# Seven-product pairs of an MLP: two accumulations continue in the banks of two others, five vector sums instead of seven

## The chip, the cores and the metric

The kernel runs on one core of one Trainium2 chip. The metric is device time in microseconds (us), the median of the runs shown. TensorE is called PE in the profile, VectorE DVE, ScalarE ACT, GpSimd POOL, SyncE SP; PEld is the loading of weights into PE. PSUM, the memory that PE writes, has eight banks here, each of which holds one result of 128 x 512 fp32 numbers.

## The reference

A decoder trunk of two layers on 256 tokens with a residual stream of 2048 numbers, all in fp32: attention with latent projections (MLA) and an MLP, then a Mamba-2 mixer and an MLP. Each of the four parts begins with an RMS norm and adds its result to the stream. The change lies in the MLPs:

```
def squared_relu_mlp(h, w_in, w_out):
    u = jax.nn.relu(h @ w_in)
    return (u * u) @ w_out
...
h = rms_norm(x, mlp_norm_g[i])
x = x + squared_relu_mlp(h, mlp_w_in[i], mlp_w_out[i])
```

with `w_in` of 2048 x 8192 and `w_out` of 8192 x 2048.

## The kernel before, in words

*fp32 by halves.* Every operand of a large product is split into a high half and a low half (`Flow.halves`, lines 102 and 103): ACT copies the raw weights, rounded, into `wh`, and DVE writes the difference into `wl`. A product of 128 x 128 by 128 x 512 then takes three matmuls, high by high, high by low and low by high (lines 616 to 618). Weights come in units of 128 x 1024 numbers (512 KB). A unit is loaded into one of six `raw` buffers by SP's queue, and split into one of four `wh` and one of four `wl` buffers. `Flow.next` loads units up to six ahead of the one that PE takes next, and splits them three ahead.

*The hidden layer in pairs.* The 8192 hidden columns are 16 blocks of 512, taken as eight pairs p. Pair 0 is computed classically. Pairs 1 to 7 are computed with seven products instead of eight: the tokens are two halves (t = 0, 1), the contraction is two halves, the columns are two blocks (j = 0, 1). The seven products M1, M2, N3, N4, N5, N6 and N7 have combinations of the activations on one side (made once per MLP, `combinations`) and of the weights on the other (made per unit on DVE at line 183, and on POOL's queue by a load that adds, line 199). Each product is four units of six matmuls. The four results come out of them by sums: with w = N6 - M1,

```
(j0, t0) = M1 + M2            (j1, t1) = N7 + N5 + w
(j0, t1) = N4 - (N7 + w)      (j1, t0) = N5 + N3 + w
```

*Banks.* N7 accumulates in a bank of the pool `sm` (2 banks, shared with the transposes); the other six take a bank of `acc` (4 banks) each when their first unit begins. `yp` (2 banks) holds the output product.

*After a product* (`after`, line 627): M1 is copied to SBUF by ACT (line 630). When both N5 and N6 are complete, DVE makes w, `c` = N5 + w, N7 + w and `e` = N7 + c; when N4, M2 or N3 is complete, one more DVE sum makes the result. `sub` is line 620 and `plus` line 621. ACT then scales and applies the ReLU (`relu_in_place`, line 624), squares (line 566), and `turn` enters the transposes of the result into a list of due times. From pair 1 to 6, POOL's queue first copies three quarters of the squared result (line 308). PE transposes them (lines 322 and 324), ACT and DVE split the transposed result (lines 299 and 300).

*Order.* PE runs in the order in which the program is written, which `plan` and `merged` make: units of the seven products, in the order of M1, N7, N5, N6 by quarter, then N4, then M2, then N3, with units of the output product (`o`, from the hidden pairs before) put in between by estimates of PE's and DVE's work. A pair's last unit of N3 is followed by two units of `o`, then by the next pair's M1 and N7, one more unit of `o`, and its N5 and N6. In pair 7, N3 follows N6 more closely, and four units of `o` come at its end. The other engines' instructions are put in order by the framework from dependencies and estimates, so that instructions that stand together in the program may be interleaved with splits. Every engine then runs its own queue in order.

Of the kernel before, what the change touches and what calls it, by code (L numbers as in the profile page):

```python
# [23 lines left out]
AF = mybir.ActivationFunctionType  # L24
# [5 lines left out]
S = 256  # L30
# [184 lines left out]
class Trunk:  # L215
# [343 lines left out]
    def mlp_body(self, mp, layer, gain):  # L559
        nc = self.nc  # L560
        xa, rs = self.xT, self.rs
        us = {}

        def hidden(r, pp, j, t):

            nc.scalar.activation(r, r, AF.Square)
            if (pp, j) not in us:
                us[pp, j] = (self.ktile(self.k4), self.ktile(self.k4))
            h, lo = us[pp, j]
            if by_words(pp, j, t):  # L570
                r = self.words(r, 3, mp)
            return lambda wide: self.transposes(r, h, lo, t, wide)

        def relu(src, t):
            r = self.scratch()
            nc.scalar.activation(r, src, AF.Relu, scale=rs[t])
            return r

        def lhs_x(kt, t):
            return [v[:, kt % 8] for v in xa[kt // 8, t]]  # L580

        def lhs_u(pp):
            return self.from_tiles([us[pp, 0], us[pp, 1]])

        S, steps = self.combinations(mp, xa)
        S["M1"], S["N4"], S["M2"] = xa[0, 0], xa[1, 1], xa[1, 0]
        out, bank, v, count = {}, {}, {}, {}
        due = []
        at = [0.0, 0.0]

        def when(us, fn):
            due.append((at[0] + us, fn))

        def move(us):
            at[0] += us
            for e in [e for e in due if e[0] <= at[0]]:
                due.remove(e)
                e[1]()

        def turn(r, p, j, t, us):  # L600

            fn = hidden(r, p, j, t)
            at[1] = max(at[0] + us + (COPY if by_words(p, j, t) else 0), at[1] + TR_GAP)
            due.append((at[1], lambda: fn(False)))

        def pair_of_banks(pool):
            return [pool.tile([P, 512], F32, tag=pool.name, name=self.name(pool.name)) for _ in range(2)]

        def products(accs, key, lhs, kt, first, last):
            u, (h, lo) = self.flow.next(key)  # L610
            for q in range(2):
                k = 2 * kt + q
                wh, wl = h[:, q * 512:(q + 1) * 512], lo[:, q * 512:(q + 1) * 512]
                for t, b in enumerate(accs):
                    ah, al = lhs(k, t)
                    nc.tensor.matmul(b, ah, wh, start=first and q == 0, stop=False)  # L616
                    nc.tensor.matmul(b, ah, wl, start=False, stop=False)  # L617
                    nc.tensor.matmul(b, al, wh, start=False, stop=last and q == 1)  # L618

        sub = lambda o, a, b: nc.vector.tensor_tensor(o, a, b, ALU.subtract)  # L620
        plus = lambda o, a, b: nc.vector.tensor_tensor(o, a, b, ALU.add)

        def relu_in_place(r, t):
            nc.scalar.activation(r, r, AF.Relu, scale=rs[t])
            return r

        def after(name, p):
            if name == "M1":
                v["m1"] = self.scratch()
                nc.scalar.activation(v["m1"], bank["M1"], AF.Copy)  # L630
            elif name in ("N5", "N6"):
                v[name] = p
                if v.get("N5") != p or v.get("N6") != p:
                    return
                w, c, e = (self.scratch() for _ in range(3))
                sub(w, bank["N6"], v["m1"])
                plus(c, bank["N5"], w)
                plus(w, bank["N7"], w)
                plus(e, bank["N7"], c)
                v["w"], v["c"] = w, c  # L640
                turn(relu_in_place(e, 1), p, 1, 1, TR[0])
            elif name == "N4":
                sub(v["w"], bank["N4"], v["w"])
                turn(relu_in_place(v["w"], 1), p, 0, 1, TR[1])
            elif name == "M2":
                plus(v["m1"], bank["M2"], v["m1"])
                turn(relu_in_place(v["m1"], 0), p, 0, 0, TR[2])
            elif name == "N3":
                plus(v["c"], bank["N3"], v["c"])
                turn(relu_in_place(v["c"], 0), p, 1, 0, TR[3])  # L650

        tokens = plan()
        inside = False
        when(5, steps[0])
        when(10, steps[1])
        for tok in tokens:
            key = (tok[0], layer) + tok[1:]
            if tok[0] == "s":
                _, p, name, d = tok
                if not inside:  # L660
                    inside = True
                    self.flow.ahead = (6, 3)
                if count.setdefault(name, 0) % 4 == 0:
                    pool = self.sm if name == "N7" else self.acc
                    bank[name] = pool.tile([P, 512], F32, tag=pool.name, name=self.name("st"))
                count[name] += 1
                products([bank[name]], key, lambda k, t: [x[:, k] for x in S[name]], d,
                         count[name] % 4 == 1, count[name] % 4 == 0)
                if count[name] % 4 == 0:
                    after(name, p)  # L670
                move(1.36)
            elif tok[0] == "c":
                _, p, j, o = tok
                if o == 0:
                    out["c"] = pair_of_banks(self.yp if j else self.acc)
                products(out["c"], key, lhs_x, o, o == 0, o == 7)
                if o == 7:
                    for t in range(2):
                        turn(relu(out["c"][t], t), p, j, t, TR[4])
                    if j:  # L680
                        when(3, steps[2])
                if o % 2:
                    self.tick()
                move(2.72)
            else:
                _, p, nb, o = tok
                if o == 0:
                    out[nb] = pair_of_banks(self.yp)
                products(out[nb], key, lhs_u(p), o, o == 0, o == 3)
                if o == 3:  # L690
                    self.add_residual(nb, out.pop(nb))
                move(2.72)
        move(1e9)
        assert not self.queue
        if gain is not None:
            self.boundary_begin(gain)
        for nb in range(4):
            keys = [("mo", layer, 7, nb, q) for q in range(2)]
            if gain is None and nb == 3:
                self.last_block(keys, lhs_u(7))  # L700
                break
            accs = self.block(keys, lhs_u(7))
            if gain is not None:
                self.finalize(nb, accs)
            else:
                for t in range(2):
                    self.result(t, nb, slice(0, 512), accs[t])
        if gain is not None:
            self.boundary_end()
# [694 lines left out]
TR = (10, 8, 7, 7, 5)  # L1404
# [4 lines left out]
def by_words(p, j, t):  # L1409

    return 0 < p < 7
# [48 lines left out]
def plan():  # L1460

    out = [("c", 0, 0, o) for o in range(8)]
    for p in range(1, 8):
        first = [(("o", p - 2, 3), 4)] if p > 1 else [(("c", 0, 1), 8)]
        out += merged(p, first + [(("o", p - 1, nb), 4) for nb in range(4 if p == 7 else 3)])
    return out
# [139 lines left out]
```

## Time and profile before

| what | us |
|---|---|
| median of 3 runs (lowest to highest) | 2285.71 (2285.32 to 2286.46) |
| the profiled execution: span from its first to its last instruction (its time beside that is not listed) | 2284.5 |
| PE busy | 2278.1 |
| PEld busy | 1889.6 |
| DVE busy | 1915.9 |
| ACT busy | 1390.1 |
| POOL busy | 275.5 |

The first MLP takes about 257 to 905 us of the span, the second about 1592 to 2240 us. In a row of a group stand: line, engine, operation, result <- operands by the program's names (`st` is a bank of one of the seven products, `s` a scratch tile, `sN` the combined activations, `xt` activations as they are, `wraw` a weight buffer), shapes, count, busy time, mean length in ns, and the engine's idle time just before, with what ended it. In a row of a timeline stand start, length, engine, line and operation; in a row of the chain of waits, start, length and what. Matmuls are pipelined: a record is longer than the step from one start to the next.

### The profile page before, as it was taken

To read this page: it belongs to the slowest core of one execution; us is meant where nothing else is said; L and a number is where in the kernel's file an instruction comes from. 1 tells how busy PE (TensorE), PEld (TensorE's weight loads), DVE (VectorE), ACT (ScalarE), POOL (GpSimd) and SP (SyncE) were. 2 spreads that over 40 slices of the span, in tenths; PEclk is the share of its full clock that TensorE was granted. 3 is DMA by queue.
4 is the path that set the end of the run, shared out by engine and by line. 5 is a ranking of instruction groups with operands and counts; after the bars stand their busy time and mean duration, and the time that the engine had idled before them with its cause. 6 is when DMAs were issued, how large, how long until landed. Compare 5 with 4: busy or idle time off the path is not lost.

```text
span 2284.5 us, 30768 instructions
## 1 busy us (share of the span) xinstructions
PE 2278.1 (100%) x10929; PEld 1889.6 (83%) x10929; DVE 1915.9 (84%) x2318; ACT 1390.1 (61%) x1947; POOL 275.5 (12%) x315
## 2 busy tenths in 40 slices
PE   9999999999999999999999999999999999999999
PEld 7898888888888888888888888888888888888887
DVE  7786698999898897687899688676989889989985
ACT  7775576566666666564666555545666666666663
POOL 1440000000000000100133213121000000000000
PEclk9999999999999999999999999999999999999999
DMA  8545678888888878667888787767688888888874
GB/s 315 173 153 159 211 230 267 259 255 270 264 255 259 267 232 271 227 208 241 277 280 278 245 275 264 229 222 229 204 265 248 259 270 253 260 275 247 267 232 160
DMA packets 167706, 557.16 MB, mean 244 GB/s; under 512 B 19040, under 2 KB 28192, under 8 KB 166528
## 3 DMA queue, kind: packets, MB, share of 16 engines
q1 hardware_dynamic: 151264, 502.44, 66.2%
q0 software_dynamic: 13888, 48.49, 10.0%
q10 hardware_dynamic: 2400, 4.27, 0.5%
q8 instruction: 86, 1.41, 0.3%
q14 instruction: 68, 0.56, 0.1%
HBM read 529.65 MB, written 6.41 MB: 235 GB/s over the span
## 4 chain that ended last, share of the span: by engine, by line
PE 96%; DVE 1%; DMA 1%; ACT 1%; issue 1%; POOL 0%; SPq 0%; ACTq 0%; DVEq 0%
PE acc L339 13%; PE acc L340 13%; PE acc L343 13%; PE yp L618 9%; PE yp L617 9%; PE yp L616 9%; PE st L617 7%; PE st L618 7%; PE st L616 7%; DMA wraw<-mi 1%; PE sm L324 1%; DVE wl L103 1%; PE y L1309 1%; PE sm L322 1%; PE acc L616 1%; PE acc L618 1%
## 5 line engine op out<-in xcount | busy, mean ns | idle before, releaser
L102 ACT ACTIVATE wh<-wraw 128x1024 fp32r<-128x1024 f32 (+1 forms) x818 | 856.2, 1053 | 570.4 <-PE acc L340 268.9
L103 DVE TENSOR_TENSOR wl<-wraw,wh 128x1024 fp32r<-128x1024 f32 (+1 forms) x818 | 985.5, 1221 | 240.6 <-ACT wh L102 216.6
L616 PE MATMUL yp<-wh,k 128*128 128x512 f32 x896 | 349.2, 390 | 0.0
L618 PE MATMUL yp<-wh,k 128*128 128x512 f32 x896 | 348.8, 389 | 0.0
L617 PE MATMUL yp<-wl,k 128*128 128x512 f32 x896 | 348.6, 389 | 0.0
L339 PE MATMUL acc<-wh,xt 128*128 128x512 f32 x704 | 279.7, 397 | 0.4 <-ACT wh L102 0.4
L340 PE MATMUL acc<-wh,xt 128*128 128x512 f32 x704 | 274.9, 390 | 0.1
L102 ACT ACTIVATE wh<-wrx 128x1024 fp32r<-128x1024 f32 x168 | 177.8, 1058 | 153.4 <-PE yp L618 101.7
L103 DVE TENSOR_TENSOR wl<-wrx,wh 128x1024 fp32r<-128x1024 f32 x168 | 204.3, 1221 | 36.6 <-ACT wh L102 35.6
L618 PEld LDWEIGHTS yp<-wh,k 128*128 128x128 f32 x896 | 168.2, 188 | 35.1
L617 PEld LDWEIGHTS yp<-wl,k 128*128 128x128 f32 x896 | 168.2, 188 | 34.9
L616 PEld LDWEIGHTS yp<-wh,k 128*128 128x128 f32 x896 | 168.2, 188 | 34.8
L339 PE MATMUL acc<-wh,k 128*128 128x512 f32 x496 | 196.5, 396 | 0.0
L340 PE MATMUL acc<-wh,k 128*128 128x512 f32 x496 | 193.3, 390 | 0.0
L343 PE MATMUL acc<-wl,xt 128*128 128x512 f32 x704 | 188.3, 389 | 0.0
L616 PE MATMUL st<-wh,xt 128*128 128x512 f32 x448 | 177.7, 397 | 0.0
L618 PE MATMUL st<-wh,xt 128*128 128x512 f32 x448 | 174.9, 390 | 0.0
L617 PE MATMUL st<-wl,xt 128*128 128x512 f32 x448 | 174.7, 390 | 0.0
L339 PEld LDWEIGHTS acc<-wh,xt 128*128 128x128 f32 x704 | 132.7, 188 | 29.4 <-ACT wh L102 1.6
L340 PEld LDWEIGHTS acc<-wh,xt 128*128 128x128 f32 x704 | 132.5, 188 | 28.5 <-issue 1.2
L343 PEld LDWEIGHTS acc<-wl,xt 128*128 128x128 f32 x704 | 132.1, 188 | 27.7
L199 POOL DMA_DIRECT2D wrx<-mi x56 | 49.2, 878 | 720.6 <-DVE wl L103 524.5
(318 smaller groups left out, 3527.0 us busy)
## 6 DMA issues: line engine op xcount, KB each, us to landing
wraw<-mi SPq DMA_DIRECT2D x256, 512.0 KB, 5.5
wraw<-mo SPq DMA_DIRECT2D x256, 512.0 KB, 5.6
wraw<-si SPq DMA_DIRECT2D x160, 512.0 KB, 5.2
wraw<-so SPq DMA_DIRECT2D x64, 512.0 KB, 5.2
wrx<-mi SPq DMA_DIRECT2D x56, 512.0 KB, 5.4
wrx<-mi POOLq DMA_DIRECT2D x56, 512.0 KB, 7.8
wraw<-wo SPq DMA_DIRECT2D x32, 512.0 KB, 4.0
taps<-xD SPq DMA_DIRECT2D x16, 768.0 KB, 8.4
```

Source lines behind the costliest of these rows:

```text
L102: self.last = nc.scalar.activation(h[:, v], raw[:, v], AF.Copy)
L103: self.last_lo = nc.vector.tensor_tensor(lo[:, v], raw[:, v], h[:, v].bitcast(F32), ALU.subtract)
L199: nc.gpsimd.dma_start(st["b11"].tile, quarter(d, 1, 0), accum_op=ALU.add)
L322: self.nc.tensor.transpose(b.bitcast(F32R)[:, v], words[:, v], self.ident_r)
L324: self.nc.tensor.transpose(b[:, v], src[:, v], self.ident)
L339: nc.tensor.matmul(accs[t][:, :n], ah, wh[:, q, :], start=first and kt + q == 0, stop=False)
L340: nc.tensor.matmul(accs[t][:, :n], al, wh[:, q, :], start=False, stop=False)
L343: nc.tensor.matmul(accs[t][:, :n], lhs(kt + q, t)[0], wl[:, q, :], start=False, stop=en and q == nk - 1)
L616: nc.tensor.matmul(b, ah, wh, start=first and q == 0, stop=False)
L617: nc.tensor.matmul(b, ah, wl, start=False, stop=False)
L618: nc.tensor.matmul(b, al, wh, start=False, stop=last and q == 1)
L1309: nc.tensor.matmul(y[t][c, o], part(t)[:, c], xg[g][t][:, o], start=True, stop=True)
```

## The change

M2 no longer takes a bank: its products go on accumulating in M1's bank, after ACT has copied M1 out, and ACT applies the ReLU to that bank directly. N3 goes on in N5's bank after the sums that need N5 have been read. The sums behind N5 and N6 become w = N6 - M1, `g` = N7 + w and `e` = N5 + g; with the one behind N4 and the one behind N3 they are five for a pair. Such continued accumulations begin without the flag that starts a sum, and their group check at build time is skipped (`more`). A pair takes four banks of `acc` in place of six. Plan, order of products, weights and due times are the same.

```diff
-        def products(accs, key, lhs, kt, first, last):
+        def products(accs, key, lhs, kt, first, last, more=False):
...
-                    nc.tensor.matmul(b, ah, wh, start=first and q == 0, stop=False)
-                    nc.tensor.matmul(b, ah, wl, start=False, stop=False)
-                    nc.tensor.matmul(b, al, wh, start=False, stop=last and q == 1)
+                    nc.tensor.matmul(b, ah, wh, start=first and q == 0, stop=False, skip_group_check=more)
+                    nc.tensor.matmul(b, ah, wl, start=False, stop=False, skip_group_check=more)
+                    nc.tensor.matmul(b, al, wh, start=False, stop=last and q == 1, skip_group_check=more)
...
-                w, c, e = (self.scratch() for _ in range(3))
+                w, g, e = (self.scratch() for _ in range(3))
                 sub(w, bank["N6"], v["m1"])
-                plus(c, bank["N5"], w)
-                plus(w, bank["N7"], w)
-                plus(e, bank["N7"], c)
-                v["w"], v["c"] = w, c
+                plus(g, bank["N7"], w)
+                plus(e, bank["N5"], g)
+                v["w"], v["g"] = w, g
                 turn(relu_in_place(e, 1), p, 1, 1, TR[0])
             elif name == "N4":
-                sub(v["w"], bank["N4"], v["w"])
-                turn(relu_in_place(v["w"], 1), p, 0, 1, TR[1])
+                sub(v["g"], bank["N4"], v["g"])
+                turn(relu_in_place(v["g"], 1), p, 0, 1, TR[1])
             elif name == "M2":
-                plus(v["m1"], bank["M2"], v["m1"])
-                turn(relu_in_place(v["m1"], 0), p, 0, 0, TR[2])
+                nc.scalar.activation(v["m1"], bank["M1"], AF.Relu, scale=rs[0])
+                turn(v["m1"], p, 0, 0, TR[2])
             elif name == "N3":
-                plus(v["c"], bank["N3"], v["c"])
-                turn(relu_in_place(v["c"], 0), p, 1, 0, TR[3])
+                plus(v["w"], bank["N5"], v["w"])
+                turn(relu_in_place(v["w"], 0), p, 1, 0, TR[3])
...
-                if count.setdefault(name, 0) % 4 == 0:
+                onto = {"M2": "M1", "N3": "N5"}.get(name, name)
+                if count.setdefault(name, 0) % 4 == 0 and onto == name:
...
-                products([bank[name]], key, lambda k, t: [x[:, k] for x in S[name]], d,
-                         count[name] % 4 == 1, count[name] % 4 == 0)
+                products([bank[onto]], key, lambda k, t: [x[:, k] for x in S[name]], d,
+                         count[name] % 4 == 1 and onto == name, count[name] % 4 == 0, onto != name)
```

## The prediction

> **What bounds the kernel now.** I read the page first: its span, its engines, the granted clock and the chain that ended last.
>
> ```profile
> span 2284.5 us, 30768 instructions
> PE 2278.1 (100%) x10929; PEld 1889.6 (83%) x10929; DVE 1915.9 (84%) x2318; ACT 1390.1 (61%) x1947; POOL 275.5 (12%) x315
> PEclk9999999999999999999999999999999999999999
> PE 96%; DVE 1%; DMA 1%; ACT 1%; issue 1%; POOL 0%; SPq 0%; ACTq 0%; DVEq 0%
> ```
>
> TensorE is busy in 2278.1 of 2284.5 us, at the full granted clock, and 96% of the chain is its own work. Next I read the busy time by stretches, cut at the two MLPs (their rows), because the change touches nothing else.
>
> ```profile
> 257.00:905.00 648.00, 647.83 (x2929) 534.61 (x2928) 581.24 (x573) 409.91 (x446) 39.63 (x56) 1.00 0.83 255
> 1592.00:2240.00 648.00, 647.90 (x2936) 534.37 (x2935) 586.86 (x579) 412.26 (x452) 38.67 (x55) 1.00 0.82 253
> ```
>
> The columns after the length are PE, weight loads, DVE, ACT and POOL. PE lacks 0.17 us in the first MLP and 0.10 us in the second; DVE has 67 and 61 us to spare. But records of matmuls overlap, so short lateness hides inside busy time. I therefore read the starts of single products in the timeline (pair 3 running into pair 4 of the first MLP), and the idle time before the weight loads in the groups by form:
>
> ```profile
> 569.32 0.39 PE L618 MATMUL st<-wh,sN 128*128 128x512 f32 x1
> 569.55 0.40 PE L616 MATMUL st<-wh,sN 128*128 128x512 f32 x1
> 570.01 0.50 PE L617 MATMUL st<-wl,sN 128*128 128x512 f32 x1
> 570.35 0.40 PE L618 MATMUL st<-wh,sN 128*128 128x512 f32 x1
> ```
>
> ```profile
> L617 PEld LDWEIGHTS st<-wl,xt 128*128 128x128 f32 x448 | 84.2, 188 | 17.2 <-DVE wl L103 0.6
> L617 PEld LDWEIGHTS st<-wl,sN 128*128 128x128 f32 x336 | 63.2, 188 | 15.2 <-DVE wl L103 2.6
> ```
>
> An undisturbed product starts 0.23 us after the one before (569.32 to 569.55), although its record is 0.39 long. At 570.01 the step is 0.46, then 0.34: the second matmul of N6's first product came 0.23 + 0.11 = 0.34 us late, since the low half `wl` of its weights was not split in time. The two load rows group all such cases of the seven products: PE waited 0.6 + 2.6 = 3.2 us for DVE's `wl`, in both MLPs together. That is the most that a quicker DVE can give back here; everything else in these stages is PE's own work at its own rate.
>
> **What a stall hangs on.** The chain of waits leading to 570.01 (start, length, what):
>
> ```profile
> 551.93 0.58 DVE s L621
> ...
> 555.40 1.23 DVE wl L103
> 556.64 6.71 DMA wraw<-mi
> ...
> 568.73 1.24 DVE wl L103
> 570.01 0.50 PE st L617
> ```
>
> Read from the end: the late `wl` (568.73) stands behind a weight load of 6.71 us, which could start only when the split at 555.40 had released its buffer, and that split stood behind a sum at 551.93, line 621. In program order that sum is M2's `plus`, one of the two that the change removes.
>
> **The change part by part.** The rows for the prices (groups by form):
>
> ```profile
> L621 DVE TENSOR_TENSOR s<-st,s 128x512 f32<-128x512 f32 x70 | 46.7, 684 | 0.1
> L624 ACT ACTIVATE s<-s,rs 128x512 f32<-128x512 f32 x56 | 40.2, 718 | 17.8 <-DVE s L621 11.4 <-DVE s L620 6.4
> L576 ACT ACTIVATE s<-acc,rs 128x512 f32<-128x512 f32 x4 | 2.7, 683 | 2.0 <-PE acc L618 2.0
> ```
>
> *Sums.* Two `plus` leave each of 7 pairs in 2 MLPs: 28 x 0.684 = 19.2 us of DVE (line 621 falls from 70 to 42). PE stands beside all of it: it hides behind 648 us of PE in each MLP. So 19.2 us is not the gain; the gain is whatever of the 3.2 us of PE's waiting goes away.
>
> *M2's ReLU.* It reads the bank instead of SBUF: count unchanged, 14 instructions on ACT at 0.683 (the row nearest, a scaled ReLU from a bank) in place of 0.718, -0.5 us on an engine with 61% load: nothing on the path. It no longer waits for a DVE sum, so it can start earlier.
>
> *Products.* The counts and the order on PE stay, as do weights, transfers, transposes and due times; the skipped group check adds no instruction. A product that continues in a bank should cost what any later product of a group costs; I bound this by the mean of the group's first and second products in the rows above, 0.39 us each way: no difference, 0.
>
> *Waits added.* PE now waits (a) before M2 for the copy of M1, (b) before N3 for the sum e out of N5's bank, (c) before the next pair's M1 for M2's ReLU, (d) before its N5 for N3's sum. Behind a waiting PE stands everything: later products, then ACT's splits waiting for PE's weight buffers. The cover is read from the timelines of the same pair (DVE sums, and then the PE rows that begin N3, the next M1 and the next N5):
>
> ```profile
> 537.56 1.28 DVE L621 TENSOR_TENSOR s<-st,s 128x512 f32<-128x512 f32 x2
> 558.80 0.68 DVE L621 TENSOR_TENSOR s<-st,s 128x512 f32<-128x512 f32 x1
> ```
>
> ```profile
> 550.96 0.48 PE L616 MATMUL st<-wh,xt 128*128 128x512 f32 x1
> 562.24 0.48 PE L616 MATMUL st<-wh,xt 128*128 128x512 f32 x1
> 568.08 0.48 PE L616 MATMUL st<-wh,sN 128*128 128x512 f32 x1
> ```
>
> (b) e ends at 537.56 + 1.28 = 538.84, N3 begins at 550.96: 12.1 us of cover. (c) M2 is done when N3 begins; with 0.68 us of ReLU the bank is free near 551.7, and M1 comes at 562.24: 10.5 us. (d) N3's sum ends at 559.48, N5 comes at 568.08: 8.6 us, filled by PE with two units of the output product, M1 and N7. (a) is as before: that copy releases the bank today too. The tightest place is pair 7, whose N3 follows soon:
>
> ```profile
> 878.66 1.28 DVE L621 TENSOR_TENSOR s<-st,s 128x512 f32<-128x512 f32 x2
> 880.46 4.62 DVE L103 TENSOR_TENSOR wl<-wraw,wh 128x1024 fp32r<-128x1024 f32 x4
> ```
>
> ```profile
> 881.45 0.39 PE L616 MATMUL st<-wh,xt 128*128 128x512 f32 x1
> 881.73 0.50 PE L617 MATMUL st<-wl,xt 128*128 128x512 f32 x1
> 882.06 0.39 PE L618 MATMUL st<-wh,xt 128*128 128x512 f32 x1
> 882.99 0.39 PE L616 MATMUL st<-wh,xt 128*128 128x512 f32 x1
> ```
>
> There e ends at 879.94 and N3 begins at 882.99: 3.05 us, and 0.6 more with one sum less ahead. All waits cost 0 as long as DVE keeps within these margins.
>
> *What comes back.* The starts of PE in both MLPs show seven late places of a kind with those quoted: five at N6's first product (the first at 570.01, the last at 2071.38) and two in pair 7 (at 881.73 and 2216.38). The last of each:
>
> ```profile
> 2071.01 0.40 PE L616 MATMUL st<-wh,sN 128*128 128x512 f32 x1
> 2071.38 0.50 PE L617 MATMUL st<-wl,sN 128*128 128x512 f32 x1
> 2071.72 0.40 PE L618 MATMUL st<-wh,sN 128*128 128x512 f32 x1
> ...
> 2216.11 0.39 PE L616 MATMUL st<-wh,xt 128*128 128x512 f32 x1
> 2216.38 0.50 PE L617 MATMUL st<-wl,xt 128*128 128x512 f32 x1
> 2216.72 0.40 PE L618 MATMUL st<-wh,xt 128*128 128x512 f32 x1
> ```
>
> At N6 the steps are 0.34 us late at the first of the five and 0.14 + 0.11 = 0.25 at the last; in pair 7, 0.05 + 0.10 = 0.15 both times. In pair 7 DVE runs without a gap from its sums into the late split, so one sum less moves the split 0.6 us and both stalls go: 2 x 0.15 = 0.3. At N6, DVE alone would also move the release at 555.40 by 0.58 us, more than the stall; but the split there needs ACT's `wh`:
>
> ```profile
> 552.64 1.06 ACT L102 ACTIVATE wh<-wraw 128x1024 fp32r<-128x1024 f32 x1 [0.19 <-PE st L618]
> 553.60 0.71 ACT L624 ACTIVATE s<-s,rs 128x512 f32<-128x512 f32 x1
> 554.22 1.04 ACT L102 ACTIVATE wh<-wraw 128x1024 fp32r<-128x1024 f32 x1
> ```
>
> That `wh` ends at 555.26, 0.14 us ahead of the split, and ACT is packed before it. If ACT keeps its order, the release moves about 0.1 us: 5 x 0.1 = 0.5 back. If the ReLU, which no longer waits for DVE, takes the idle 0.19 us, the release moves up to 0.3 us and all five stalls go: 5 x 0.3 (between 0.34 and 0.25) = 1.5. I take the middle, 1.0, since nothing in the rows decides ACT's order. Late next would be the same split, now with a tenth or two to spare.
>
> Sum: 0 (products) + 0 (waits) - 0.3 - 1.0 = -1.3 us. The page gives the profiled execution only its span, 2284.5; the runs' median, 2285.71 (2285.32 to 2286.46), lies 1.2 above. So 2283.2 for the span, and 2285.7 - 1.3 = **2284.4 us** for the median. Bounds: 3.2 back at best (2282.5), and 0 back (2285.7).
>
> **Rivals.**
>
> *Nothing comes back.* The load of 6.71 us or ACT's order keeps the five stalls, pair 7 gives 0.3 or less: 2285.4 to 2285.7. For it speaks ACT's `wh` ending 0.14 us before the split; against it, the removed sum stands on the chain itself.
>
> *DVE is the bound* (faster). If PE were only following DVE, 19.2 us would come off: 2266.5. For it: DVE is busy 84% of the span, and in the chain its sum stands ahead of a stall. Against it: DVE has 67 and 61 us of slack in the MLP stretches, and PE waited for `wl` for 3.2 us only. [...]
>
> *A bank comes free too late* (slower). Four accumulator banks now hold four sums per pair, and N5's bank is closed until N3's sum is read. If DVE issues that sum only behind the splits and buffer sums of the next pair, later than 568.08 and so 8.6 us or more later than now, PE stands at N5 for it: 0.68 for the sum and 0.11 to get going again, 0.79 x 12 pair boundaries = 9.5 us, 2295.2. For it: DVE's order is mixed by a planner (splits lie between the sums), and DVE does stand in a queue there. Against it: 8.6 us are seven splits. [...]
>
> *Five sums are not what arrives*: were M2 to overwrite the bank, times would be those of the forecast, and only values differ. This has no time of its own.
>
> **How the numbers follow.** Forecast 0.61, nothing back 0.25, DVE the bound 0.04, a late bank 0.07, some other disturbance of the order within 3 us above 0.03. A measurement here tells 0.2%, 4.6 us, from no change. Forecast, nothing and the small disturbance lie within it: same 0.89; faster 0.04; slower 0.07. The range goes from 2282.0 (all 3.2 back, and the runs' own 0.4 below the median) to 2288.0 (nothing back, with a few new stalls of 0.3 us); it leaves out the two far rivals.
>
> **What would show it.** Right: line of sums 42 + 28, DVE about 1897 us busy, PE unchanged near 2278; the load row for `st<-wl,sN` waiting less than 2.6 us for `wl`; the step at N6's first product nearer 0.23 than 0.46. The ReLU step is wrong if its row from `st` is above 0.72 us, the bank step if a PE product of N5, M1 or N3 waits for DVE or ACT at lines 616 to 618. The whole is wrong if the MLP stretches differ from 648 us by more than 2 us each.

## The result: 1.4% slower, and the profile after

The changed kernel takes 2315.28 us (median of 4 runs, 2314.45 to 2322.1), the kernel before beside it 2286.03 us: a ratio of 1.0136, with a 95% interval of 1.0122 to 1.0149. The forecast was 2284.4 us. The profiled execution spans 2313.5 us, 29.0 more than before. First its page, with the span, the busy time of the engines and the chain that ended last by engine:

```profile
span 2313.5 us, 30732 instructions
PE 2284.4 (99%) x10929; PEld 1892.7 (82%) x10929; DVE 1903.9 (82%) x2290; ACT 1388.2 (60%) x1947; POOL 274.8 (12%) x315
PE 94%; DMA 3%; DVE 1%; issue 1%; ACT 1%; POOL 0%; DVEq 0%; SPq 0%; ACTq 0%
```

The sums are gone as planned: DVE has 28 instructions fewer. PE has as many instructions as before, but is busy 6.3 us longer (2284.4 against 2278.1), and transfers hold 3% of the chain where they held 1%. The stretches of the two MLPs, which now last longer (columns as before: length, PE, weight loads, DVE, ACT, POOL):

```profile
257.00:920.00 663.00, 651.49 (x2928) 536.51 (x2927) 574.77 (x558) 408.50 (x446) 39.54 (x56) 0.99 0.81 250
1607.00:2268.00 661.00, 649.29 (x2934) 534.75 (x2933) 579.78 (x564) 411.07 (x451) 38.58 (x55) 1.00 0.81 247
```

In 648 us PE lacked 0.17 and 0.10 us before. Now it lacks 663.00 - 651.49 = 11.5 us in the first MLP and 661.00 - 649.29 = 11.7 in the second. Which instruction waits is told by the groups by form (busy time and mean ns, then idle time before and what ended it):

```profile
L617 PE MATMUL st<-wl,xt 128*128 128x512 f32 x448 | 176.4, 394 | 23.2 <-DVE wl L103 23.2
L617 PEld LDWEIGHTS st<-wl,sN 128*128 128x128 f32 x336 | 63.2, 188 | 13.0 <-DVE wl L103 0.4
L621 DVE TENSOR_TENSOR s<-st,s 128x512 f32<-128x512 f32 x42 | 28.7, 684 | 0.1
L645 ACT ACTIVATE s<-st,rs 128x512 f32<-128x512 f32 x14 | 9.6, 689 | 2.1 <-PE st L618 1.1
```

The first row is the whole of what PE lacks: 23.2 us before second matmuls of products whose activations are `xt` (N3's are among them), and always for DVE's low half `wl`. The second row is the wait that was to shrink, and it did: 2.6 us before, 0.4 now. The list of waits says how often it happens and what DVE itself waits for (total, times, longest), after and then before:

```profile
DVE wraw L183 <- DMA wraw<-mi: 40.6, 26, 3.5
PE st L617 <- DVE wl L103: 23.2, 10, 3.1
```

```profile
DVE wraw L183 <- DMA wraw<-mi: 18.1, 27, 2.0
```

There are ten places. By the starts of PE's instructions they are the same place ten times: the last of N3's four units, in pairs 2 to 6 of both MLPs. Line 183 is the sum of two weight buffers, and DVE's waiting there for loads has grown from 18.1 to 40.6 us. Here is pair 3 of the first MLP, DVE's timeline before and then after:

```profile
550.79 1.23 DVE L103 TENSOR_TENSOR wl<-wraw,wh 128x1024 fp32r<-128x1024 f32 x1
551.93 0.68 DVE L621 TENSOR_TENSOR s<-st,s 128x512 f32<-128x512 f32 x1
552.53 0.68 DVE L300 TENSOR_TENSOR k<-sm,k 128x512 fp32r<-128x512 f32 x1
553.13 3.49 DVE L103 TENSOR_TENSOR wl<-wraw,wh 128x1024 fp32r<-128x1024 f32 x3
556.53 1.22 DVE L183 TENSOR_TENSOR wraw<-wraw,wraw 128x1024 f32<-128x1024 f32 x1
```

```profile
554.89 1.23 DVE L103 TENSOR_TENSOR wl<-wraw,wh 128x1024 fp32r<-128x1024 f32 x1
556.21 0.69 DVE L300 TENSOR_TENSOR k<-sm,k 128x512 fp32r<-128x512 f32 x1
559.00 1.23 DVE L183 TENSOR_TENSOR wraw<-wraw,wraw 128x1024 f32<-128x1024 f32 x1 [2.10 <-DMA wraw<-mi]
560.14 3.49 DVE L103 TENSOR_TENSOR wl<-wraw,wh 128x1024 fp32r<-128x1024 f32 x3
```

M2's sum (551.93) is missing, as it should. But line 183 has moved as well: the sum that makes the next pair's first weights for N7 stood behind three splits and now stands ahead of them. There DVE waits 2.10 us for its load, from 556.90 to 559.00, and runs nothing else meanwhile: the three splits behind the sum wait with it. Their own data are there when the sum is through (the last of ACT's three `wh` ends at 559.53), and at 560.14 they start and run in one go (3.49 us, as before). PE in the same place, before and then after:

```profile
555.40 0.39 PE L617 MATMUL st<-wl,xt 128*128 128x512 f32 x1
```

```profile
555.06 0.48 PE L616 MATMUL st<-wh,xt 128*128 128x512 f32 x1
...
559.28 0.39 PE L616 MATMUL st<-wh,xt 128*128 128x512 f32 x1
561.42 0.50 PE L617 MATMUL st<-wl,xt 128*128 128x512 f32 x1 [1.75 <-DVE wl L103]
```

The arithmetic closes. N3 began at 550.96 before (the prediction's row) and begins at 555.06 now, 4.10 us later, through the stall of pair 2. Set against that, the three splits start 560.14 - 553.13 - 4.10 = 2.91 us later than they did. Before, the first of them ended near 553.13 + 1.22 = 554.35 and PE took it at 555.40: 1.05 us of cover. So PE should be 2.91 - 1.05 = 1.86 us late, and it is: 561.42 - 559.28, less the usual step of 0.23, is 1.91.

The balance of the span: 23.2 us of PE waiting and 6.3 us of longer PE work are 29.5, against 29.0 measured. PE's instructions stand in the same order in both kernels, so their starts can be compared one by one: 31.1 us are lost at and just behind the ten places, and 2.1 us are regained elsewhere, 1.8 of them at N6 and in pair 7.

### The profile page after: what moved, and what is told of

It reads as the page before. It is cut to its first block, busy times and chain, and to the rows that moved or that the text cites. A ratio compares the mean times of both kernels' runs of the same rounds, so it can differ in the third digit from the quotient of the medians.

```text
span 2313.5 us, 30732 instructions
## 1 busy us (share of the span) xinstructions
PE 2284.4 (99%) x10929; PEld 1892.7 (82%) x10929; DVE 1903.9 (82%) x2290; ACT 1388.2 (60%) x1947; POOL 274.8 (12%) x315
## 4 chain that ended last, share of the span: by engine, by line
PE 94%; DMA 3%; DVE 1%; issue 1%; ACT 1%; POOL 0%; DVEq 0%; SPq 0%; ACTq 0%
PE acc L339 13%; PE acc L340 13%; PE acc L343 13%; PE yp L616 9%; PE yp L617 9%; PE yp L618 9%; PE st L617 7%; PE st L618 7%; PE st L616 7%; DMA wraw<-mi 2%; DVE wl L103 1%; PE sm L324 1%; PE y L1309 1%; PE sm L322 1%; PE acc L616 1%
## 5 line engine op out<-in xcount | busy, mean ns | idle before, releaser
L617 PE MATMUL st<-wl,xt 128*128 128x512 f32 x448 | 176.4, 394 | 23.2 <-DVE wl L103 23.2
L339 PEld LDWEIGHTS acc<-wh,xt 128*128 128x128 f32 x704 | 132.6, 188 | 29.3 <-ACT wh L102 1.1
```

The lines of the kernel that those rows point to most:

```text
L339: nc.tensor.matmul(accs[t][:, :n], ah, wh[:, q, :], start=first and kt + q == 0, stop=False)
L617: nc.tensor.matmul(b, ah, wl, start=False, stop=False, skip_group_check=more)
```

## The experiments

Theory A: what costs the time is the order of DVE's queue, the load-dependent sum at line 183 ahead of the splits. Theory B, the rival: the continued banks themselves hold something up. DVE's order at a pair's end, read from each kernel's program, helps to follow the runs (l a split of raw weights, m the split for M1, k a split of transposed values, r a residual sum, + a sum of results, 7 the sum at line 183 for N7's first unit):

```
before                l r r l + k l l l 7 m +
after                 l r r l   k 7 l l l m +
one column of a sum   l r r l + l k 7 l l m +
128 columns           l r r l + l k l 7 l m +
```

In DVE's order of pairs 2 to 6, the change differs from the kernel before in two things only: the removed sums, and the place of 7 at the ten pair ends. One split in pair 1 of each MLP moved as well; PE does not wait there.

**Each half alone.** The first kernel continues M2 in M1's bank and leaves N3 and its sums as before; the second continues N3 in N5's bank and leaves M2.

```diff
-                onto = {"M2": "M1", "N3": "N5"}.get(name, name)
+                onto = {"M2": "M1"}.get(name, name)      # m2_alone, with N3's four sums as before
+                onto = {"N3": "N5"}.get(name, name)      # n3_alone, with M2's sum as before
```

> Only M2 continues in M1's bank and loses its sum; N3 keeps a bank and a sum of its own, six sums per pair. In the order built for DVE, the buffer sum of the next pair's N7 (line 183) then stands ahead of the three splits that follow M2, as in the changed kernel. Theory A (DVE's order: that buffer sum waits for a weight load and holds N3's last split behind it): the whole loss is here, ten late products at N3's fourth unit, 2313 to 2317 us. Theory B (banks held too long): about half of the loss or less, since the bank of N5 is free as before, 2290 to 2305.

> Only N3 continues in N5's bank, with the sums regrouped; M2 keeps its bank and its sum, six sums per pair. DVE's order is that of the kernel before, with one sum less behind N6. Theory A: no loss, 2284.5 to 2286.0. Theory B: the bank that is needed soonest by the next pair is N5's, so half of the loss or more, 2295 to 2310.

M2 alone: 2319.1 us, ratio 1.014 (1.0127 to 1.0154). N3 alone: 2285.5 us, 0.9997 (0.9989 to 1.0006). The list of waits of M2 alone:

```profile
PE st L617 <- DVE wl L103: 24.7, 10, 2.8
```

The whole loss comes with M2's half, at ten places again, some 2 us above the expected range. N3's half removes 14 sums of DVE and continues a bank, and the interval of its time holds 1.

**No bank continued, M2's sum left out.** The kernel before, but ACT reads M2's own bank. Block (j0, t0) is then the ReLU of M2 alone, without M1.

```diff
-                plus(v["m1"], bank["M2"], v["m1"])
-                turn(relu_in_place(v["m1"], 0), p, 0, 0, TR[2])
+                nc.scalar.activation(v["m1"], bank["M2"], AF.Relu, scale=rs[0])
+                turn(v["m1"], p, 0, 0, TR[2])
```

> The kernel before with all six banks, the order and waits of its banks untouched; only the sum behind M2 is left out and the ReLU is applied to M2's own bank, so that the block (j0, t0) lacks M1. In the order built for DVE the first buffer sum of N7 then stands ahead of the three splits, as in the changed kernel. Theory A (DVE's order): the whole loss without any bank continued, 2312 to 2320 us, ten late products at N3's fourth unit. Theory B (banks): no loss, 2284 to 2287.

2318.59 us, 1.0143 (1.013 to 1.0157). Every product has its own bank as before, and the loss is there in full. Its timeline of DVE at pair 3 shows the same picture as the changed kernel:

```profile
559.80 1.22 DVE L183 TENSOR_TENSOR wraw<-wraw,wraw 128x1024 f32<-128x1024 f32 x1 [2.81 <-DMA wraw<-mi]
560.94 3.49 DVE L103 TENSOR_TENSOR wl<-wraw,wh 128x1024 fp32r<-128x1024 f32 x3
```

**Both banks continued, a sum put back.** The changed kernel with a sum at M2's place whose result nobody reads. It costs DVE what M2's sum cost.

```diff
             elif name == "M2":
+                junk = self.scratch()
+                plus(junk, bank["M1"], v["m1"])
                 nc.scalar.activation(v["m1"], bank["M1"], AF.Relu, scale=rs[0])
```

> The changed kernel with both banks continued and five sums, and beside them one more DVE sum of the same size where M2's was, whose result nobody uses. The order built for DVE is then that of the kernel before. Theory A: the loss is gone, 2284.5 to 2286.5, though the bank of M1 is even read once more. Theory B: the loss stays, 2313 or more.

2286.44 us, 0.9999 (0.999 to 1.0008). DVE's timeline:

```profile
551.97 0.68 DVE L621 TENSOR_TENSOR s<-st,s 128x512 f32<-128x512 f32 x1
552.57 0.68 DVE L300 TENSOR_TENSOR k<-sm,k 128x512 fp32r<-128x512 f32 x1
553.17 3.49 DVE L103 TENSOR_TENSOR wl<-wraw,wh 128x1024 fp32r<-128x1024 f32 x3
556.57 1.22 DVE L183 TENSOR_TENSOR wraw<-wraw,wraw 128x1024 f32<-128x1024 f32 x1
```

The old order is back, to 0.04 us, and with it the old time, although DVE does 14 useless sums. These two runs settle A against B: banks as before and the new order is slow, banks continued and the old order is not.

**The order kept without the sum.** The changed kernel, with the sum at line 183 for the first quarter (d == 0) written into M1's unit and tied behind the last split that was written before it.

```diff
             if name == "N7":
-                add("b22", "b12", "b22")
+                if not (d == 0):
+                    add("b22", "b12", "b22")
...
+            if name == "M1" and (d == 0):
+                with flow.tc.issue_after(flow.los[-1].ins):
+                    add("b22", "b12", "b22")
```

(`flow.los` keeps the last splits.)

> The changed kernel in full, five sums and both banks continued; only the first buffer sum of each pair's N7 (line 183) is written into the program one unit earlier and tied behind the split before, so that it stands behind the three splits again, as in the kernel before. Theory A: the loss is gone and the late products at N6 and in pair 7, which the changed kernel no longer shows, stay away: 2283.0 to 2285.5. Theory B: 2313 or more.

2289.09 us, 1.0012 (1.0003 to 1.0021). The stall at N3 is gone and about 26 of the 29 us are back, but the time is 3.6 us above the range that A gave. PE now waits elsewhere, in N5 and in units of the output product (the lines lie seven and one further down in this kernel). Its list of waits, and one of DVE's waits behind them:

```profile
PE st L624 <- DVE wl L104: 3.1, 3, 1.4
PE yp L624 <- DVE wl L104: 1.7, 4, 0.5
```

```profile
664.40 1.23 DVE L185 TENSOR_TENSOR wraw<-wraw,wraw 128x1024 f32<-128x1024 f32 x1 [2.47 <-DMA wraw<-mi]
665.54 1.22 DVE L185 TENSOR_TENSOR wrx<-wrx,wraw 128x1024 f32<-128x1024 f32 x1
```

With the first sum tied, the framework orders the later buffer sums of the pair anew. At 664.40 one that waits 2.47 us for its load stands ahead of one that came first in the kernel before:

```profile
663.13 1.22 DVE L183 TENSOR_TENSOR wrx<-wrx,wraw 128x1024 f32<-128x1024 f32 x1
...
665.44 1.22 DVE L183 TENSOR_TENSOR wraw<-wraw,wraw 128x1024 f32<-128x1024 f32 x1
```

It is the same mechanism in small. That this order is the whole of the remainder wasn't undone by itself.

**How far behind.** If the position in the queue is the cause, the cost should follow it. A useless sum of one column, or of 128, is enough to shift the order by one or two splits, and costs DVE 0.15 or 0.28 us.

```diff
+                junk = self.scratch()
+                plus(junk[:, :1], bank["M1"][:, :1], v["m1"][:, :1])        # one_split_ahead
+                plus(junk[:, :128], bank["M1"][:, :128], v["m1"][:, :128])  # two_splits_ahead
```

> The changed kernel in full, with one extra DVE sum of a single column behind M2, whose result nobody uses. In the order built for DVE, N7's first buffer sum then stands behind one of the three splits (N3's last) and ahead of two. Theory A: N3 is no longer late; the split behind the sum belongs to the output unit that PE takes 1.36 us later, so each of the ten stalls shrinks from about 2.5 to 0.5 to 1.2 us: 2289 to 2298.

> The same with an extra sum of 128 columns: the buffer sum stands behind two splits and ahead of one, whose unit PE takes 4.1 us after N3's last. Theory A: that is longer than DVE waits, so hardly a stall is left: 2284 to 2288. In both runs Theory B (banks held too long) expects 2313 or more.

| of the three splits, ahead of the sum at line 183 | us | ratio (95%) | DVE waits there for loads, us |
|---|---|---|---|
| none (the change) | 2315.28 | 1.0136 (1.0122 to 1.0149) | 40.6 |
| one (one column) | 2304.27 | 1.0078 (1.0066 to 1.0091) | 41.6 |
| two (128 columns) | 2290.2 | 1.0014 (1.0005 to 1.0023) | 29.3 |
| three (order_kept, no extra work) | 2289.09 | 1.0012 (1.0003 to 1.0021) | 32.8 |
| three (sum_kept, 512 columns) | 2286.44 | 0.9999 (0.999 to 1.0008) | 19.7 |

With one split ahead N3 gets its weights in time and the next split is late, for the output unit behind N3. The timeline of DVE and the wait of PE:

```profile
553.38 1.22 DVE L103 TENSOR_TENSOR wl<-wraw,wh 128x1024 fp32r<-128x1024 f32 x1
554.52 0.68 DVE L300 TENSOR_TENSOR k<-sm,k 128x512 fp32r<-128x512 f32 x1
556.59 1.23 DVE L183 TENSOR_TENSOR wraw<-wraw,wraw 128x1024 f32<-128x1024 f32 x1 [1.39 <-DMA wraw<-mi]
557.73 2.35 DVE L103 TENSOR_TENSOR wl<-wraw,wh 128x1024 fp32r<-128x1024 f32 x2
```

```profile
PE yp L617 <- DVE wl L103: 11.7, 11, 1.8
```

With two ahead that row falls to:

```profile
PE yp L617 <- DVE wl L103: 0.9, 3, 0.5
```

DVE waits as long with one split ahead as with none (41.6 and 40.6 us), and yet the time is 11 us lower. Some 5 us of that are PE's longer work, which is missing with one split ahead (PE is busy 2279.5 us, against 2284.4); most of the rest is that PE waits less. So DVE's waiting alone doesn't tell the cost: it matters who stands behind it and how much cover that one has. Both runs lie above their expectations, by 6 and by 2 us; in both, PE also waits before two transposes (2.9 and 2.1 us), which the expectations did not have.

**Ways around it.** Four more kernels try to keep the gain with another cure. The first gives N7's first operand, loaded for this sum, a buffer pool of its own, so that it need not wait for a raw buffer; it was also put into the kernel before, as a measure of what the pool itself does.

```diff
-            for name, n in (("rx", 4), ("ry", 1)):
+            for name, n in (("rx", 4), ("ry", 1), ("rz", 2)):
...
-B12 = "raw"
+B12 = "rz"
```

> The changed kernel, with two weight buffers of their own for N7's first operand instead of taking them from the six of wraw; N7's buffer sum still stands ahead of the three splits in DVE's order. Loads can start a unit or more earlier. Theory A in the form that the wait for the load is what costs: DVE waits less or not at all at line 183, most of the loss goes, 2284 to 2294. If instead the place of the sum costs by itself (1.2 us in front of three splits, without any wait): ten products late by about a microsecond, 2293 to 2300. Theory B: 2313 or more.

> The control for the run above: the kernel before with the same two buffers; the place of N7's first buffer sum is behind the splits. Earlier loads can only take the seven late products of 0.15 to 0.34 us: 2283.5 to 2286.5, unless the planner's order puts another wait in front of a split.

2311.0 us, 1.0102 (1.0087 to 1.0118) on the change, and 2288.72, 1.0011 (1.0002 to 1.002) on the kernel before, where the pool helped nothing either; that is 2.2 us above the range expected for it. The first lies above both ranges of Theory A, and its time alone would be nearer to B's. But PE waits in it as in the changed kernel (20.3 us before second matmuls, for `wl`), and sum_left_out and sum_kept had ruled B out. The first missed since its premise did not come true: the other operand still comes through `wraw`, and the sum moved one place further ahead, to where it waits longest. Its timeline of DVE:

```profile
557.38 1.22 DVE L183 TENSOR_TENSOR wraw<-wrz,wraw 128x1024 f32<-128x1024 f32 x1 [3.36 <-DMA wraw<-mi]
558.53 0.68 DVE L300 TENSOR_TENSOR k<-sm,k 128x512 fp32r<-128x512 f32 x1
```

The second ties the sum behind a split without moving it in the program; it then lands behind N3's sum, later than ever before.

```diff
-                add("b22", "b12", "b22")
+                with flow.tc.issue_after(flow.los[-2].ins) if d == 0 else nullcontext():
+                    add("b22", "b12", "b22")
```

> The changed kernel in full; the first buffer sum of each pair's N7 is tied behind the split of the unit two before, and in the order built for DVE it then stands behind the three splits, M1's split and N3's sum, some 2 us later than in the kernel before. Theory A: no late product at N3, but N7 and N6 of the next pair come closer to late: 2284 to 2292. Theory B: 2313 or more.

2293.45 us, 1.003 (1.0018 to 1.0041): no stall at N3, but N5 and output units wait now and then for what comes later; 1.5 us above the expected range.

The third and fourth load both operands of the sum four units earlier, into a pool of two buffers of their own; the fourth also has the order of order_kept.

```diff
+        for i, u in enumerate(self.units):
+            if u.key[0] == "s" and u.key[2:] == (u.key[2], "N7", 0) and u.key[2] > 1:
+                self.units[i - 4].loads += u.loads
+                u.loads = []
...
-                 "N7": lambda: [load("b12", B12, (0, 1)), load("b22", "raw", (1, 1))],
+                 "N7": lambda: [load("b12", B12 if d else "rz", (0, 1)), load("b22", "raw" if d else "rz", (1, 1))],
```

> The changed kernel with both operands of each pair's first N7 unit in two buffers of their own, and their loads written four units earlier. The planner then puts the loads and the buffer sum (line 183) into the pair before, far from the three splits that follow M2. Theory A (a buffer sum that waits for its load holds N3's split): nothing waits in front of N3's last split, the ten late products go, 2282.5 to 2288, with five sums and both banks continued. Theory B (banks held too long): 2313 or more. The run own_buffers did not test this, since there DVE waited for the other operand in wraw just as long.

> As the run above, but with the buffer sum written one unit earlier and tied behind the split before, as in order_kept: it stands behind the three splits, and its loads have come long before. Theory A: no wait at this sum at all; what is left of order_kept's loss comes from the later buffer sums of the pair, 2283 to 2289.

2298.99 us, 1.0055 (1.0043 to 1.0068), and 2288.79, 1.0008 (0.9999 to 1.0018). Alone, the earlier load missed: the framework put the sum earlier still, into the pair before, where it waits for the earlier load. From the list of waits (line 183 is 187 here):

```profile
DVE wrz L187 <- DMA wrz<-mi: 15.8, 10, 5.7
```

With the order tied as well, the time is near that of order_kept and not below it: the loads were not what remained.

No kernel here beats the kernel before by more than the noise: the fastest, N3's half alone, is 0.03% below it, with an interval that holds 1.

## Why the prediction was wrong

**The step that failed** is the one that priced the order at nothing. In the prediction's part on products it reads that the order on PE stays, "as do weights, transfers, transposes and due times", and in the part on what comes back, "one sum less moves the split 0.6 us". Both take DVE's remaining instructions to keep their order and to close up by what was removed. PE's order did stay. DVE's is made by the framework from dependencies and estimates, so taking one instruction out is also a new input to that ordering. The text knew this ("DVE's order is mixed by a planner") but used it only for the late bank. There was a chance of 0.03 for "some other disturbance of the order within 3 us"; it was the right kind at a tenth of its size.

The price could have been bounded from rows of before. The first of the three splits had 1.05 us of cover (553.13 + 1.22 to 555.40), the sum directly behind them takes a step of 1.14 us on DVE (it starts at 556.53, the next split at 557.67), and sums of its line waited up to 2.0 us for a load in the list of waits, though this one had no wait where it stood. Ahead of the splits it costs up to 1.14 + 2.0 less 0.60 for the missing sum less 1.05 of cover, 1.5 us, at each of ten pair ends: some 15 us as an estimate, without what follows a stall. Measured: 23.2 us of waits, and 6.3 of longer work.

**What else went as it was said, and what not:**

- *Sums.* The counts were right (the row of line 621 is at 42), the size a little high: DVE is busy 12.0 us less, not 19.2. The records overlap by 0.08 us (551.93 to 552.53 is a step of 0.60), which makes 28 x 0.60 = 16.8; the rest was not followed. They were hidden: N3's half takes 14 of them away and moves the time by nothing that can be told.
- *ReLU from the bank.* Right: 689 ns in 14 instructions, against 683 forecast.
- *Waits added, rival of the late bank.* Right that they cost 0: sum_kept has all four waits and the time of the kernel before. No product waits for a bank. The sign named for this step, a product of N3 that waits for DVE at lines 616 to 618, did come up, but the wait is for `wl`: read by its engine and line alone, that sign can't tell a bank from a weight.
- *What comes back.* The places were right and the size a little low: 1.8 us were regained at N6 and in pair 7, against 1.3, and the wait of `st<-wl,sN` fell from 2.6 to 0.4 us. The changed kernel alone doesn't show why, since its stalls at N3 also give DVE time; order_kept, which has no stall at N3, has 1.9 us back at the seven places. The halves tell them apart: N6 stays late at some places where M2's sum is kept and the buffers are as before (n3_alone, sum_kept: `st<-wl,sN` waits 2.3 and 2.9 us there), and pair 7 stays 0.15 us late where N3's sums are kept (m2_alone, sum_left_out). At N6 the larger of the two values weighed, 1.5, came; by which of the two ways ACT went was not followed. The loss elsewhere buries it.
- *DVE is the bound.* Refuted: 1915.9 us of work became 1903.9 and the time rose. DVE's share of busy time did not tell what bounds the kernel: N3's half takes 14 sums off DVE and the ratio is 0.9997, and sum_kept with 14 useless sums is 29 us faster than the change without them.
- *The sign that the whole is wrong* (MLP stretches more than 2 us off) came up in both MLPs, and its row, PE's wait for `wl`, is the one that the prediction read for the gain. It had bounded what could be won there (3.2 us), and not what could be lost.

What stays open: by which of its estimates the framework moved the sum. The runs show the order in each case and that the length of one instruction decides it, not the reckoning. Open too is the remainder of 2 to 3 us in order_kept.

## What to carry to other kernels

Where a framework orders the queues, taking an instruction away can also change the order: before forecasting, look for the load-dependent instruction that stands next behind the gap, and compare the wait it would bring to the front with the cover of what it would overtake. Hidden work may be what holds a queue in a good order, so read the queue of an engine off the critical path in both traces, instruction by instruction, before believing that a saving there is free. An experiment that puts the removed time back as useless work (sum_kept) and one that removes the time alone (sum_left_out) tell an effect of order from the effect of the change itself.

## What was not expected of the hardware

PE did not always come back from a wait at its old rate. Three of the ten places, by PE's timeline of the changed kernel; the first two with what follows (pairs 2 and 4 of the first MLP), the third (second MLP) alone:

```profile
474.60 0.79 PE L617 MATMUL st<-wl,xt 128*128 128x512 f32 x1 [2.27 <-DVE wl L103]
475.20 0.63 PE L618 MATMUL st<-wh,xt 128*128 128x512 f32 x1
475.62 0.63 PE L616 MATMUL st<-wh,xt 128*128 128x512 f32 x1
...
648.05 0.50 PE L617 MATMUL st<-wl,xt 128*128 128x512 f32 x1 [3.11 <-DVE wl L103]
648.39 0.40 PE L618 MATMUL st<-wh,xt 128*128 128x512 f32 x1
648.63 0.56 PE L616 MATMUL st<-wh,xt 128*128 128x512 f32 x1
648.98 0.63 PE L617 MATMUL st<-wl,xt 128*128 128x512 f32 x1
...
1995.54 0.50 PE L617 MATMUL st<-wl,xt 128*128 128x512 f32 x1 [2.02 <-DVE wl L103]
```

Behind the first wait the records are 0.63 us long at once, in place of 0.39, and the steps between them 0.43 instead of 0.23; behind the second this begins 0.6 us later, behind the third 1.6 us later. The stretches behind the waits of pairs 2, 3 and 4 and of that third place (columns as above; the granted clock is the third from the end):

```profile
474.60:478.00 3.40, 3.40 (x8) 2.72 (x9) 3.40 (x4) 0.86 (x1) 0.00 (x0) 0.50 0.63 178
561.40:565.00 3.60, 3.58 (x16) 2.93 (x17) 3.60 (x4) 1.06 (x1) 0.00 (x0) 1.00 0.63 179
648.50:652.00 3.50, 3.50 (x11) 2.71 (x10) 3.50 (x5) 1.06 (x1) 0.00 (x0) 0.53 0.84 226
1997.10:2000.50 3.40, 3.40 (x10) 2.71 (x9) 3.40 (x4) 0.97 (x1) 0.00 (x0) 0.52 0.89 293
```

For some 3.4 us the granted clock is half: 0.50 from 474.62 to 478.03, from 648.70 to 652.11 and from 1996.97 to 2000.38 us. It happened behind three of the ten waits, those of 2.27, 3.11 and 2.02 us, and not behind the other seven, though four of those were longer than two of the three (2.33 to 2.77 us). Some eight steps at 0.20 us more each are 1.6 us, for three places about 5 us as an estimate: most of the 6.3 us by which PE's busy time grew. A wait of 2.02 us had a stretch at half clock behind it here, and one of 2.77 had none, so the length of a wait alone doesn't tell where one follows. The stretch begins 0.02 us behind the end of the first wait, and 0.65 and 1.43 us behind the other two. What decides this is left open here.
